# Tiles moved to the weights' address modulo 2048, and a bias table copied from DRAM instead of from SBUF: a two-layer decoder trunk

## The chip, the cores and the metric

One core of one Trainium2 chip runs the whole program. The time is device time in microseconds (us) of one execution; lower is better. The inputs and the outputs are in the chip's DRAM. The other names below are those of the profile: PE is TensorE's matmul, PEld its weight load, DVE is VectorE, ACT is ScalarE, POOL is GpSimd, SP is SyncE, whose queue issues most of the DMAs.

## The reference

The input is 512 tokens of width 1024. All is float32.

```python
def reference(x, ...):
    # layer 0
    x = x + hgrn2_mixer(rmsnorm(x, g0), w_in, w_out, ...)     # 8 heads, gated linear recurrence
    x = x + conv_ffn(rmsnorm(x, g1), w_up, conv, w_down)      # 1024 -> 2 x 2816 -> 1024
    # keys and values of layer 1 come from the stream here
    k, v = split(rmsnorm(x, g2) @ kv_w)
    # layer 1
    x = x + diff_attention(rmsnorm(x, g3), k, v, w_q, w_o, rel_table, ...)
    x = x + conv_ffn(rmsnorm(x, g4), w_up, conv, w_down)
    return rmsnorm(x, g5)

def conv_ffn(h, w_up, conv_w, conv_b, w_down):
    u = causal_depthwise_conv3(h @ w_up) + conv_b
    gate, val = split(u)
    return (silu(gate) * val) @ w_down

# diff_attention: per head two score maps, each softmax(q_c @ k_c.T + bias), out = (p_0 - lam * p_1) @ v;
# bias[h, i, j] = rel_table[t5_bucket(i - j), h], minus infinity where j > i
```

## The kernel before

**Layout.** The stream x is kept transposed: 8 tiles `x0` to `x7` of 128 channels by 512 tokens. A float32 product is made of three products of the rounded type F32R: each operand is split into a high and a low part, and `mm3` (lines 102 to 104) issues high by high, high by low, low by high. An operand that is split is named `..h` and `..l`: `xh`, `xl` for the normed stream, `yh`, `yl` for a mixer's output before its out-projection, `hh`, `hl` for the inner layer of the FFN (`hid` in the code, 22 pairs), `whi`, `wlo` for weights, `kh`, `kl` and `qs` for keys and queries.

**One matmul.** A projection's matmul has 128 columns of a weight tile as the stationary operand (512 bytes of each partition) and a whole 512-token tile as the moving operand (2048 bytes of each partition). One output tile takes 8 k-tiles by 3 matmuls from the stream, and 22 by 3 in the down-projection (`residual`). Values are the other way round: the weights move, 256 columns at a time, and the stream is stationary.

**Where tiles lie.** Pools are laid one behind the other in SBUF in the order in which they are opened: `const`, `weights`, `xsplit`, `small`, and then one pool per stage (`hgrn`, `ffn0`, `attn`, `ffn1`), each from where `small` ends. A pool's tags stand in the order of their first use, and every buffer is rounded up to 32 bytes. `weights` holds nine buffers of 4096 bytes and `xsplit` sixteen of 2048, so weights and the split stream have the same address modulo 2048. `small` ends with 22 buffers of 32 bytes, so the stages begin 704 bytes past that place. In `ffn` three tiles `u` of 2056 bytes (2080 when rounded up) come first, so `hid` begins 704 + 3 x 32 = 800 bytes past it. In `hgrn` the outputs `ys` come behind `dl`, `lb`, `om`, `scd`, `sd`, `oacc`, so 704 + 96 + 1024 = 1824 bytes past it. In `attn` the outputs `ys` begin 704 bytes past it, and keys and queries 160 bytes further.

**Weights.** `stage` (line 79) issues the DMA of a 512 KB weight tile into one of three `wst` buffers, all on SP's queue; `split` makes `whi` with ACT (line 57) and `wlo` with DVE (line 58), into three buffers each. In the attention, `Load` does the same with lines 756 and 759, and POOL multiplies the gain in (line 84).

**Order.** A scheduler orders `hgrn` and `ffn` from the program's order. The first matmuls, the attention and the last tile are in hand-written order. In `hgrn`, head h's projections and `prep` run ahead of the score products of head h - 1 (`intra`), and the gate's projection of head h - 2 fills in.

**The bias.** At head 2, `bias_vector` (line 702) makes a vector of 383 numbers for each of the 8 heads, in partitions 0 to 7 of one SBUF tile (`bvec`), and one DMA on SP's queue (line 711) writes each vector 128 times into a DRAM table, `bdram`, of 8 x 128 x 383 numbers: 1024 rows of 1532 bytes, 1.57 MB. The attention reads it at an offset that grows by one for each row (line 743), some 550 us later.

Of the kernel before, what the change touches and what calls it, by code (L numbers as in the profile page):

```python
# [11 lines left out]
F32 = mybir.dt.float32  # L12
F32R = mybir.dt.float32r
# [6 lines left out]
P = 128  # L20
T = 512
D = 1024
KD = D // P
NH = 8
DFF = 2816
KF = DFF // P
# [3 lines left out]
U0, U1, U2, U3 = 8, 2, 3, 1  # L30
PIECES = {0: 1, 1: 3, 3: 6, 6: 8}
WARM = 8


class Trunk:
# [237 lines left out]
    def hgrn(self, xs, acc, on_tile):  # L273
        tc, nc, a, sp = self.tc, self.nc, self.a, self.sp
        v, s = nc.vector, nc.scalar
        with ExitStack() as ctx:
            hp = ctx.enter_context(tc.tile_pool(name="hgrn", bufs=1))
            self.banks(ctx, "hgrn", mm=(4, 1), at=(4, 1))
            f_ps, q_ps = self.bank(), self.bank()
            self.begin(xs, acc, f_ps, q_ps)  # L280
            rb, rc = self.rstd(self.sums(acc, "at"), "n0", "at")
# [10 lines left out]
            for t in scd + sd:  # L292
                nc.gpsimd.memset(t, 0.0)
            oacc = hp.tile([P, T], F32, tag="oacc", name="oacc")
            ys = [(hp.tile([P, T], F32R, tag=f"yh{h}", name=f"yh{h}"),
                   hp.tile([P, T], F32R, tag=f"yl{h}", name=f"yl{h}")) for h in range(NH)]

            def big(tag, name, bufs):
                return hp.tile([P, T], F32, tag=tag, name=name, bufs=bufs)
# [203 lines left out]
            vt, pr, o = {}, {}, {}  # L503
# [145 lines left out]
    def ffn(self, layer, xs, acc, on_tile, final=None):  # L649
        tc, nc, a = self.tc, self.nc, self.a  # L650
        v, s = nc.vector, nc.scalar
        with ExitStack() as ctx:
            fp = ctx.enter_context(tc.tile_pool(name=f"ffn{layer}", bufs=1, reuse_waits="tile"))
            self.banks(ctx, f"ffn{layer}", mm=(8, 1))
            us = [fp.tile([P, T + 2], F32, tag=f"u{i}", name=f"u{i}") for i in range(3)]
            for u in us:
                nc.gpsimd.memset(u[:, 0:2], 0.0)
            hid = [(fp.tile([P, T], F32R, tag=f"hh{j}", name=f"hh{j}"),
                    fp.tile([P, T], F32R, tag=f"hl{j}", name=f"hl{j}")) for j in range(KF)]
            count = 0  # L660

            def conv(ps, n):
                nonlocal count
                u = us[count % 3]
                count += 1
                w = lambda i: self.cw[:, layer, i, n:n + 1]
                v.tensor_tensor(u[:, 2:], ps, rb, ALU.mult)  # L667
                c = fp.tile([P, T], F32, tag="c", name="c", bufs=3)
                s.activation(c, u[:, 2:], AF.Identity, bias=self.cb[:, layer, n:n + 1], scale=w(2))  # L669
                v.scalar_tensor_tensor(c, u[:, 1:T + 1], w(1), c, ALU.mult, ALU.add)  # L670
                v.scalar_tensor_tensor(c, u[:, 0:T], w(0), c, ALU.mult, ALU.add)  # L671
                return c

            def pair(j, pg, pv):
                cg = conv(pg, j)
                s.activation(cg, cg, AF.Silu)
                cv = conv(pv, KF + j)
                v.tensor_tensor(cv, cv, cg, ALU.mult)  # L678
                self.split(cv, *hid[j])

            up = a["w_up"][layer]
            first = [(self.bank("mm"), self.weights(up[n])) for n in range(3)]
            steps, got = self.norm_steps(acc, f"f{layer}", "mm")
            self.proj_first(first, xs, KD - 1, (lambda: None,) + steps)
            rb = got[1][0]
            ps3 = self.bank("mm")
            self.proj(ps3, self.weights(up[3]), xs, range(KD))
            pair(0, first[0][0], first[1][0])
            pair(1, first[2][0], ps3)
            for j in range(2, KF):  # L690
                pp = []
                for n in (2 * j, 2 * j + 1):
                    ps = self.bank("mm")
                    self.proj(ps, self.weights(up[n]), xs, range(KD))
                    pp.append(ps)
                pair(j, *pp)
            self.residual(a["w_down"][layer], hid, KF, on_tile, final=final)


    def bias_vector(self):  # L700

        nc, a = self.nc, self.a
        tab = self.sp.tile([P, T], F32, tag="sq", name="btab", bufs=2)
        nc.scalar.dma_start(tab[0:32, 0:NH + 384], a["rel"])
        u = self.sp.tile([P, T], F32, tag="sq", name="bvec", bufs=2)
        nc.scalar.dma_start(u[0:NH, 0:384], a["c_far"])
        ps = self.bank("at")
        nc.tensor.matmul(ps[:NH, :384], tab[0:32, 0:NH], tab[0:32, NH:NH + 384], start=True, stop=True)
        nc.vector.tensor_tensor(u[0:NH, 0:384], u[0:NH, 0:384], ps[:NH, :384], ALU.subtract)
        self.bdram = self.dp.tile([NH, P, 383], F32, tag="bdram", name="bdram")  # L710
        nc.sync.dma_start(self.bdram, u[0:NH, 0:383].unsqueeze(1).broadcast_to([NH, P, 383]))


    def attention(self, xkv, acc, on_tile):
        tc, nc, a = self.tc, self.nc, self.a
        v, s = nc.vector, nc.scalar
        mm = nc.tensor.matmul
        with ExitStack() as ctx:
            ap = ctx.enter_context(tc.tile_pool(name="attn", bufs=2, reuse_waits="tile"))
            self.banks(ctx, "attn", mm=(2, 1), sc=(4, 1), tp=(1, 1), po=(1, 1))  # L720
            def minus_lambda():
                lm = ap.tile([64, 4], F32, tag="lm", name="lm", bufs=1)
                nc.sync.dma_start(lm, a["lam"])
                pr = ap.tile([64, 2], F32, tag="lmp", name="lmp", bufs=1)
                v.tensor_tensor(pr, lm[:, 0:4:2], lm[:, 1:4:2], ALU.mult)
                pl = self.bank("mm")
                mm(pl[:, 0:2], self.ones[0:64, :], pr, start=True, stop=True)
                e = ap.tile([P, 2], F32, tag="lme", name="lme", bufs=1)
                s.activation(e, pl[:, 0:2], AF.Exp)
                d = ap.tile([P, 1], F32, tag="lmd", name="lmd", bufs=1)  # L730
                v.tensor_tensor(d, e[:, 1:2], e[:, 0:1], ALU.subtract)
                lam = ap.tile([P, 1], F32, tag="lam", name="lam", bufs=1)
                v.tensor_scalar(lam, d, -LAMBDA_INIT, None, ALU.add)
                return lam

# [72 lines left out]
            lam = minus_lambda()  # L808
# [140 lines left out]
            def scores(b):  # L949
                h, i = divmod(b, 4)  # L950
                if i == 0:
                    heads[h] = [ap.tile([P, 2, 4], F32, tag="sums", name="sums"),
                                ap.tile([P, 4], F32, tag="r0", name="r0"),
                                ap.tile([P, 4], F32, tag="oms", name="oms")]
                n = (i + 1) * P
                oi = slice(i * P, n)
                sc = [self.bank("sc")[:, :n] for c in range(2)]
                st = ap.tile([P, 2], F32, tag="stat", name="stat", bufs=4)
                pt = ap.tile([P, 2, T], F32, tag="p", name="p")
                for c in range(2):  # L960
                    mm(sc[c], qs[h][:, c, oi], ks[h][0][:, c, 0:n], start=True, stop=False)
                    mm(sc[c], qs[h][:, c, oi], ks[h][1][:, c, 0:n], start=False, stop=True)
                for c in range(2):
                    v.tensor_tensor_reduce(sc[c], sc[c], nbs[h // 2][:, h % 2, T - n:], 1.0, 3e38, ALU.add, ALU.min,  # L964
                                           st[:, c:c + 1])
                blocks[b] = pt

                def powers():
                    for c in range(2):
                        s.activation(pt[:, c, :n], sc[c], AF.Exp, bias=st[:, c:c + 1], scale=-1.0,  # L970
                                     accum_out=heads[h][0][:, c, i:i + 1])
                return powers

            def weigh(b):

                h, i = divmod(b, 4)
                n = (i + 1) * P
                sums, r0 = heads[h][:2]
                pt = blocks.pop(b)
                r1 = ap.tile([P, 2], F32, tag="r1", name="r1", bufs=4)  # L980
                v.reciprocal(r1[:, 0:1], sums[:, 1, i:i + 1])
                v.reciprocal(r0[:, i:i + 1], sums[:, 0, i:i + 1])
                v.scalar_tensor_tensor(r1[:, 1:2], sums[:, 0, i:i + 1], r1[:, 0:1], lam, ALU.mult, ALU.mult)
                at = blocks[b] = ap.tile([P, T], F32, tag="at", name="at")
                v.scalar_tensor_tensor(at[:, :n], pt[:, 1, :n], r1[:, 1:2], pt[:, 0, :n], ALU.mult, ALU.add)
# [24 lines left out]
            def close(h):  # L1010

                sums, r0, ms, po = heads.pop(h)
                o = ap.tile([P, T], F32, tag="o", name="o")
                me = ap.tile([P, 4], F32, tag="ome", name="ome")
                r = ap.tile([P, 4], F32, tag="or", name="or")
                by_token = o.rearrange("p (i x) -> p i x", i=4)

                def turn_back():
# [230 lines left out]
```

## Time and profile before

| what | value |
|---|---|
| median of 3 runs | 1283.47 us (1282.53 to 1287.66) |
| the profiled execution | 1283.88 us, span 1282.0 us |
| PE busy | 1246.9 us, 97% of the span |
| PEld busy | 1045.2 us, 82% |
| DVE busy | 869.2 us, 68% |
| ACT busy | 567.9 us, 44% |
| POOL busy | 111.1 us, 9% |
| DMA | 115.35 MB, mean 90 GB/s |

The span is that of the instructions; the execution's own time lies 1.9 us above it. Busy time of PE overstates its work, since matmuls are pipelined: each lasts some 0.39 us and the next begins some 0.23 us after it. So the pace of PE is read from start to start, or from the number of matmuls in a stretch, and not from its busy share.

### The profile page before, as it was taken

Reading aid. Unit: us, or ns where it says so; the run is one execution under the profiler, and the core shown is the slowest. Engines: PE = TensorE matmul, PEld = TensorE weight load, DVE = VectorE, ACT = ScalarE, POOL = GpSimd, SP = SyncE. Lnnn points to the kernel's source line nnn. Section 1 sums busy time; section 2 is a strip of 40 time slices with the busy share of each in tenths; the row PEclk is TensorE's granted clock in tenths of the full one; section 3 lists DMA queues with packets and bytes.
Section 4 is the critical chain, followed back from the end, with each engine's and each line's share of the span. In section 5 each row is a group of like instructions: output and inputs, shape, how many; then the busy total and the mean of one; then the engine's idle time right before and its main releaser. Section 6 shows DMA issues by size and latency. Waiting matters only on the chain.

```text
span 1282.0 us, 18032 instructions
## 1 busy us (share of the span) xinstructions
PE 1246.9 (97%) x6994; PEld 1045.2 (82%) x6994; DVE 869.2 (68%) x1627; ACT 567.9 (44%) x986; POOL 111.1 (9%) x93
## 2 busy tenths in 40 slices
PE   8999899999999999999999899999999999999997
PEld 7888698778888888888878788798788888888886
DVE  7978689676877777533357888876687777762223
ACT  5554455454444444322235546554454444442221
POOL 3000000020000000001143432200200000000001
PEclk9999899999999999999999899999999999999998
DMA  6225322132333333233322221222232333333321
GB/s 208 83 85 81 102 67 84 50 115 83 99 99 99 99 99 99 82 100 91 97 76 83 74 67 58 66 83 67 89 107 96 92 96 97 99 91 90 95 86 66
DMA packets 37949, 115.35 MB, mean 90 GB/s; under 512 B 4032, under 2 KB 9448, under 8 KB 37864
## 3 DMA queue, kind: packets, MB, share of 16 engines
q1 hardware_dynamic: 36968, 113.29, 29.6%
q8 instruction: 55, 0.90, 0.3%
q10 hardware_dynamic: 896, 0.92, 0.2%
q14 instruction: 30, 0.25, 0.1%
HBM read 110.52 MB, written 3.67 MB: 89 GB/s over the span
## 4 chain that ended last, share of the span: by engine, by line
PE 53%; issue 30%; DVE 11%; ACT 3%; DMA 2%; POOL 0%; SPq 0%; POOLq 0%; ACTq 0%; DVEq 0%
PE mm L103 15%; PE mm L102 15%; PE mm L104 15%; DMA wst<-in_w_fqg_dram 2%; DVE wlo L759 1%; DVE kl L857 1%; PE po L1005 1%; DVE wlo L58 1%; ACT whi L756 1%; DVE sd L457 1%; DVE sc L964 1%; PE tp L992 1%; DVE qs L840 1%; ACT p L970 0%; ACT whi L57 0%
## 5 line engine op out<-in xcount | busy, mean ns | idle before, releaser
L102 PE MATMUL mm<-xh,whi 128*128 128x512 f32 x1008 | 399.6, 396 | 0.4 <-ACT whi L57 0.4
L103 PE MATMUL mm<-xl,whi 128*128 128x512 f32 x1008 | 396.4, 393 | 3.0 <-DVE xl L61 2.9
L104 PE MATMUL mm<-xh,wlo 128*128 128x512 f32 x1008 | 396.0, 393 | 1.1 <-DVE wlo L58 1.1
L58 DVE TENSOR_TENSOR wlo<-wst,whi 128x1024 fp32r<-128x1024 f32 (+2 forms) x182 | 215.7, 1189 | 165.8 <-ACT whi L57 163.4
L57 ACT CAST whi<-wst 128x1024 fp32r<-128x1024 f32 (+2 forms) x182 | 181.8, 1003 | 257.9 <-PE mm L103 192.4
L103 PEld LDWEIGHTS mm<-xl,whi 128*128 128x128 f32 x1008 | 191.0, 190 | 42.4 <-DVE xl L61 4.5
L104 PEld LDWEIGHTS mm<-xh,wlo 128*128 128x128 f32 x1008 | 190.7, 189 | 42.2 <-DVE wlo L58 2.3
L102 PEld LDWEIGHTS mm<-xh,whi 128*128 128x128 f32 x1008 | 191.0, 190 | 38.8 <-ACT whi L57 1.2
L102 PE MATMUL mm<-hh,whi 128*128 128x512 f32 (+1 forms) x374 | 142.8, 382 | 0.0
L103 PE MATMUL mm<-hl,whi 128*128 128x512 f32 (+1 forms) x374 | 142.6, 381 | 0.0
L104 PE MATMUL mm<-hh,wlo 128*128 128x512 f32 (+1 forms) x374 | 142.6, 381 | 0.0
L667 DVE TENSOR_TENSOR u<-mm,rbc_f 128x512 f32<-128x512 f32 x88 | 60.2, 688 | 73.4 <-PE mm L104 73.4
L147 POOL TENSOR_TENSOR acc<-acc,sq 128x512 f32<-128x512 f32 x18 | 26.7, 1482 | 664.2 <-ACT sq L146 664.1
L102 PEld LDWEIGHTS mm<-hh,whi 128*128 128x128 f32 x374 | 70.1, 188 | 15.2
L104 PEld LDWEIGHTS mm<-hh,wlo 128*128 128x128 f32 x374 | 70.1, 188 | 15.2
L103 PEld LDWEIGHTS mm<-hl,whi 128*128 128x128 f32 x374 | 70.1, 188 | 15.1
L669 ACT ACTIVATE c<-u,pack 128x512 f32<-128x512 f32 x88 | 71.5, 816 | 7.7 <-DVE u L667 4.0
L102 PE MATMUL mm<-whi,xh 128*128 128x256 f32 x256 | 73.8, 290 | 0.0
L103 PE MATMUL mm<-wlo,xh 128*128 128x256 f32 x256 | 72.5, 283 | 0.6 <-DVE wlo L759 0.6
L57 ACT CAST hh<-c 128x512 fp32r<-128x512 f32 x44 | 27.2, 619 | 102.9 <-DVE c L678 102.9
L104 PE MATMUL mm<-whi,xl 128*128 128x256 f32 x256 | 72.4, 283 | 0.0
L671 DVE SCALAR_TENSOR_TENSOR c<-u,pack,c 128x512 f32<-128x512 f32 x88 | 66.1, 752 | 2.7
(259 smaller groups left out, 1717.0 us busy)
## 6 DMA issues: line engine op xcount, KB each, us to landing
wst<-in_w_up_dram SPq DMA_DIRECT2D x88, 512.0 KB, 3.6
wst<-in_w_down_dram SPq DMA_DIRECT2D x32, 512.0 KB, 3.5
wst<-in_w_fqg_dram SPq DMA_DIRECT2D x22, 512.0 KB, 4.1
wst<-in_w_kq_dram SPq DMA_DIRECT2D x16, 512.0 KB, 3.6
wst<-in_w_down_dram SPq DMA_DIRECT2D x16, 384.0 KB, 3.2
wst<-in_w_i_dram SPq DMA_DIRECT2D x8, 512.0 KB, 4.2
wst<-in_w_ao_dram SPq DMA_DIRECT2D x8, 512.0 KB, 4.0
wst<-in_w_v_dram SPq DMA_DIRECT2D x8, 512.0 KB, 3.6
```

What stands on the lines that cost most here:

```text
L57: i = nc.scalar.copy(hi, x)
L58: j = nc.vector.tensor_tensor(lo, x, hi.bitcast(F32), ALU.subtract)
L102: mm(out, s[0], m[0], start=start, stop=False)
L103: mm(out, s[0], m[1], start=False, stop=False)
L104: mm(out, s[1], m[0], start=False, stop=stop)
L147: add = lambda engine=nc.vector: engine.tensor_tensor(acc, acc, sq, ALU.add)
L457: v.copy_predicated(dst, m, src)
L667: v.tensor_tensor(u[:, 2:], ps, rb, ALU.mult)
L669: s.activation(c, u[:, 2:], AF.Identity, bias=self.cb[:, layer, n:n + 1], scale=w(2))
L671: v.scalar_tensor_tensor(c, u[:, 0:T], w(0), c, ALU.mult, ALU.add)
L756: s.copy(me.w[0], me.st)
L759: v.tensor_tensor(me.w[1], me.st, me.w[0].bitcast(F32), ALU.subtract)
```

## The change

Two things. First, tiles change their place. `ys` of `hgrn` and `hid` of `ffn` are made first in their pools. The attention's small tiles go from its own pool to `small`, and one of them gets 152 idle columns (`FILL`), so that `small` ends 2048 bytes past a multiple of 2048 from the weights (704 bytes, 640 for the padded `lm`, 704 for the others). The stages then begin at the weights' place modulo 2048, and `ys`, `hid`, `kh`, `kl` and `qs` lie there. Second, the bias vector goes to DRAM once (`once`, 12 KB), and the table is written from this copy, DRAM to DRAM, with a wait for the first DMA between the two. The arithmetic and the order of the calls stay.

```diff
+FILL = 152
@@ hgrn
             self.banks(ctx, "hgrn", mm=(4, 1), at=(4, 1))
+            ys = [(hp.tile([P, T], F32R, tag=f"yh{h}", name=f"yh{h}"),
+                   hp.tile([P, T], F32R, tag=f"yl{h}", name=f"yl{h}")) for h in range(NH)]
             f_ps, q_ps = self.bank(), self.bank()
...
             oacc = hp.tile([P, T], F32, tag="oacc", name="oacc")
-            ys = [(hp.tile([P, T], F32R, tag=f"yh{h}", name=f"yh{h}"),
-                   hp.tile([P, T], F32R, tag=f"yl{h}", name=f"yl{h}")) for h in range(NH)]
@@ ffn
+            hid = [(fp.tile([P, T], F32R, tag=f"hh{j}", name=f"hh{j}"),
+                    fp.tile([P, T], F32R, tag=f"hl{j}", name=f"hl{j}")) for j in range(KF)]
             us = [fp.tile([P, T + 2], F32, tag=f"u{i}", name=f"u{i}") for i in range(3)]
             for u in us:
                 nc.gpsimd.memset(u[:, 0:2], 0.0)
-            hid = [(fp.tile([P, T], F32R, tag=f"hh{j}", name=f"hh{j}"),
-                    fp.tile([P, T], F32R, tag=f"hl{j}", name=f"hl{j}")) for j in range(KF)]
@@ bias_vector
+        once = self.dp.tile([NH, 383], F32, tag="bonce", name="bonce")
+        nc.sync.dma_start(once, u[0:NH, 0:383])
         self.bdram = self.dp.tile([NH, P, 383], F32, tag="bdram", name="bdram")
-        nc.sync.dma_start(self.bdram, u[0:NH, 0:383].unsqueeze(1).broadcast_to([NH, P, 383]))
+        nc.sync.dma_start(self.bdram, once.unsqueeze(1).broadcast_to([NH, P, 383]))
@@ attention
-                lm = ap.tile([64, 4], F32, tag="lm", name="lm", bufs=1)
+                lm = self.sp.tile([64, 4 + FILL], F32, tag="lm", name="lm", bufs=1)[:, :4]
...
-                    heads[h] = [ap.tile([P, 2, 4], F32, tag="sums", name="sums"),
-                                ap.tile([P, 4], F32, tag="r0", name="r0"),
-                                ap.tile([P, 4], F32, tag="oms", name="oms")]
+                    heads[h] = [self.sp.tile([P, 2, 4], F32, tag="sums", name="sums"),
+                                self.sp.tile([P, 4], F32, tag="r0", name="r0"),
+                                self.sp.tile([P, 4], F32, tag="oms", name="oms")]
...
```

The lines left out do the same with `lmp`, `lme`, `lmd`, `lam`, `stat`, `r1`, `ome` and `or`.

## Rows read from the trace of the kernel before

**Rows 1.** Busy time in two stretches: HGRN, and most of the attention
```profile
core 0: us, PE busy (x) PEld busy (x) DVE busy (x) ACT busy (x) POOL busy (x), PEclk, DMA share, GB/s
0.00:250.00 250.00, 238.08 (x2171) 205.85 (x2171) 200.37 (x511) 127.67 (x270) 10.89 (x16) 0.98 0.36 97
...
650.00:850.00 200.00, 187.25 (x1123) 163.81 (x1121) 161.71 (x393) 108.67 (x278) 63.66 (x45) 0.97 0.22 69
```

**Rows 2.** The chain that ended last, in order of time: start us, us, what
```profile
81.78 0.67 PE at L439 x6
...
109.35 27.74 DMA wst<-in_w_fqg_dram
```

**Rows 3.** Waits, 94 to 140 us: total us, times, longest
```profile
ACT whi L57 <- DMA wst<-in_w_fqg_dram: 10.5, 1, 10.5
```

**Rows 4.** PE in order of time, 136 to 149 us: start us, us, what
```profile
136.37 0.39 PE L102 MATMUL mm<-xh,whi 128*128 128x512 f32 x1
142.05 1.65 PE L439 MATMUL at<-vt,kt 128*128 128x128 f32 x6 [5.29 <-ACT kt L436]
143.35 0.77 PE L103 MATMUL mm<-xl,whi 128*128 128x512 f32 x1
...
147.76 0.63 PE L104 MATMUL mm<-xh,wlo 128*128 128x512 f32 x1
148.19 0.44 PE L102 MATMUL mm<-xh,whi 128*128 128x512 f32 x1
```

**Rows 5.** DMA issues: KB each, median us from issue to landing
```profile
wst<-in_w_fqg_dram SPq DMA_DIRECT2D x22, 512.0 KB, 4.1
...
out_dram<-fin SPq DMA_DIRECT2D x6, 256.0 KB, 2.3
```

**Rows 6.** SP's queue in order of time, 94 to 135 us
```profile
101.52 0.83 SPq L711 DMA_DIRECT2D bdram<-bvec  x1
109.35 14.26 SPq L79 DMA_DIRECT2D wst<-in_w_fqg_dram  x3
```

**Rows 7.** Stretches (columns as in rows 1): table being written, stall, output being written
```profile
104.00:114.00 10.00, 10.00 (x49) 8.34 (x48) 10.00 (x29) 6.37 (x14) 0.00 (x0) 1.00 0.45 50
...
136.00:142.00 6.00, 0.76 (x4) 0.30 (x2) 3.68 (x7) 3.45 (x6) 0.00 (x0) 0.95 0.49 165
142.00:148.00 6.00, 5.95 (x17) 4.99 (x18) 6.00 (x23) 2.38 (x8) 0.00 (x0) 0.50 0.33 116
1272.00:1280.00 8.00, 1.72 (x8) 1.24 (x8) 4.07 (x22) 1.19 (x3) 1.57 (x3) 0.67 0.58 194
```

**Rows 8.** Stretches without a pause, weight loads alone: us, busy (count), PEclk, DMA
```profile
310.00:510.00 200.00, 165.62 (x883) 1.00 0.33 100
545.00:645.00 100.00, 80.31 (x429) 1.00 0.32 95
272.00:292.00 20.00, 16.12 (x86) 1.00 0.27 79
```

**Rows 9.** Same for the second FFN, all engines (columns as in rows 1)
```profile
955.00:1125.00 170.00, 170.00 (x752) 140.76 (x751) 123.38 (x157) 77.06 (x95) 0.00 (x0) 1.00 0.32 98
1155.00:1255.00 100.00, 100.00 (x433) 80.45 (x432) 29.03 (x31) 26.85 (x32) 0.00 (x0) 1.00 0.30 87
```

**Rows 10.** Groups of matmuls by line and shape: count, busy us, mean ns
```profile
L102 PE MATMUL mm<-hh,whi 128*128 128x512 f32 x330 | 130.4, 395 | 0.0
...
L102 PE MATMUL mm<-yh,whi 128*128 128x512 f32 x88 | 36.1, 410 | 0.0
...
L102 PE MATMUL mm<-hh,whi 128*128 128x256 f32 x44 | 12.5, 283 | 0.0
...
L102 PE MATMUL sc<-yh,whi 128*128 128x512 f32 x24 | 9.6, 402 | 0.0
...
L102 PE MATMUL at<-yh,whi 128*128 128x512 f32 x16 | 6.4, 411 | 0.0
```

**Rows 11.** Waits of PE, 640 to 910 us (columns as in rows 3)
```profile
PE tp L992 <- DVE at L985: 9.2, 5, 2.7
```

More of the change, by code (lines that the diff above doesn't have):

```diff
@@ L721, in minus_lambda @@
             def minus_lambda():
-                lm = ap.tile([64, 4], F32, tag="lm", name="lm", bufs=1)
+                lm = self.sp.tile([64, 4 + FILL], F32, tag="lm", name="lm", bufs=1)[:, :4]
                 nc.sync.dma_start(lm, a["lam"])
-                pr = ap.tile([64, 2], F32, tag="lmp", name="lmp", bufs=1)
+                pr = self.sp.tile([64, 2], F32, tag="lmp", name="lmp", bufs=1)
                 v.tensor_tensor(pr, lm[:, 0:4:2], lm[:, 1:4:2], ALU.mult)
@@ L727, in minus_lambda @@
                 mm(pl[:, 0:2], self.ones[0:64, :], pr, start=True, stop=True)
-                e = ap.tile([P, 2], F32, tag="lme", name="lme", bufs=1)
+                e = self.sp.tile([P, 2], F32, tag="lme", name="lme", bufs=1)
                 s.activation(e, pl[:, 0:2], AF.Exp)
-                d = ap.tile([P, 1], F32, tag="lmd", name="lmd", bufs=1)
+                d = self.sp.tile([P, 1], F32, tag="lmd", name="lmd", bufs=1)
                 v.tensor_tensor(d, e[:, 1:2], e[:, 0:1], ALU.subtract)
-                lam = ap.tile([P, 1], F32, tag="lam", name="lam", bufs=1)
+                lam = self.sp.tile([P, 1], F32, tag="lam", name="lam", bufs=1)
                 v.tensor_scalar(lam, d, -LAMBDA_INIT, None, ALU.add)
@@ L957, in scores @@
                 sc = [self.bank("sc")[:, :n] for c in range(2)]
-                st = ap.tile([P, 2], F32, tag="stat", name="stat", bufs=4)
+                st = self.sp.tile([P, 2], F32, tag="stat", name="stat", bufs=4)
                 pt = ap.tile([P, 2, T], F32, tag="p", name="p")
@@ L979, in weigh @@
                 pt = blocks.pop(b)
-                r1 = ap.tile([P, 2], F32, tag="r1", name="r1", bufs=4)
+                r1 = self.sp.tile([P, 2], F32, tag="r1", name="r1", bufs=4)
                 v.reciprocal(r1[:, 0:1], sums[:, 1, i:i + 1])
@@ L1013, in close @@
                 o = ap.tile([P, T], F32, tag="o", name="o")
-                me = ap.tile([P, 4], F32, tag="ome", name="ome")
-                r = ap.tile([P, 4], F32, tag="or", name="or")
+                me = self.sp.tile([P, 4], F32, tag="ome", name="ome")
+                r = self.sp.tile([P, 4], F32, tag="or", name="or")
                 by_token = o.rearrange("p (i x) -> p i x", i=4)
```

## The prediction

> **What bounds the kernel now.** I read the busy shares first, then the stretches by stage, the chain that ended last, and the waits. PE is busy 97% of the span and DVE 68%, so a microsecond counts only where PE loses it. The stretches show where that is: in HGRN PE is busy 238.08 of 250 us, in the attention 187.25 of 200, with a granted clock of 0.98 and 0.97 [rows 1]; both FFNs run without a gap [rows 9]. The chain shows one piece out of scale: a weight tile that took 27.74 us from issue to landing [rows 2], where its kind takes 4.1 [rows 5]. Behind it stands one wait of ACT, 10.5 us [rows 3], then a hole of PE of 5.29 us [rows 4] and a stretch at half clock [rows 7]. The second thing to see is PE's pace where nothing waits: 883 weight loads in 200 us are 226.5 ns for each matmul of the up-projection; 429 in 100 us are 233.1 in the down-projection; 86 in 20 us are 232.6 in the out-projection of HGRN [rows 8]. The second FFN repeats it: 751 loads in 170 us, 226.4, and 432 in 100, 231.5 (a few loads of half width shorten the mean, and one load too many stands in each stretch) [rows 9]. All these are matmuls of 512 columns at full clock.
>
> **The table's copy.** It is issued at 101.52 [rows 6] and reads 8 partitions of SBUF. While it runs alone, the DMA engines move 50 GB/s with 0.45 of 16 busy [rows 7]: 7.2 engines at 6.9 GB/s each. 1.57 MB at 50 GB/s are 31.4 us, from about 102.5 to 134. The weight tile issued at 109.35 stands behind it, and SP's three issues from there took 14.26 us together [rows 6], so the queue was backed up. The tile lands at 109.35 + 27.74 = 137.1, and ACT, which has waited for it since 126.6 (137.1 less 10.5 [rows 3]), splits it then.
>
> What this costs PE, from its rows in order of time [rows 4]: the last matmul before the hole starts at 136.37 and would be followed at 136.60. The clock is back at full speed with the matmul of 148.19. In these 11.59 us PE did six matmuls of line 439, which take 0.67 us in the head before [rows 2], and 11 of 512 columns (143.35 to 147.76, every 0.43 us), which take 2.50 us at 227 ns. [...] DVE is at 80% over the stage [rows 1], so it has room to do its part of this work earlier.
>
> How fast is the copy from DRAM? No row shows DRAM to DRAM. Reading weights from DRAM runs at 165 GB/s with 0.49 of 16 engines busy, 21 GB/s an engine; writing the output to DRAM at 194 with 0.58, again 21 [rows 7]. If reading and writing overlap, 7.2 engines move 151 GB/s: 10.4 us. If each row is read and then written, half that: 20.8 us. The lower end of the gain is that writing these rows, and not reading them, is what is slow: 31.4 us again. I take 10.4, since the plain rows on both sides are three times as fast as this copy, and what is different in it is the 8 source partitions. The wait for `once` is a DMA of 12 KB into DRAM; output DMAs land in 2.3 us [rows 5]. So the table's copy is issued near 104, starts near 105, and ends near 115.5, or 126 if serial. SP stands still for those 2.3 us; the next weight issue behind it comes at 109.35 [rows 6], when its buffer is free, so nothing is held. That tile then lands 2 us behind the copy, near 117.5, nine before ACT turns to it at 126.6. No stall is left up to a copy of some 20 us; serial copying leaves about 1 us. Gain: **8.4 us**, with ends 0 (less the 2.5 us that the copy starts later) and 8.4.
>
> [...]
>
> **The place of the tiles.** In the up-projection the moving tiles (`xh`, `xl`) lie at the weights' place modulo 2048; `hid` lies 800 bytes off, `ys` of HGRN 1824, `ys` of the attention 704. Shape, clock and order of the three products are the same. The difference in pace is 233.1 - 226.5 = 6.6 ns. DVE is busier in the faster stretch, 123.38 of 170 us against 29.03 of 100 [rows 9], and so is the DMA by a little, so neighbours' work doesn't explain it. I take it that place does, and that moved tiles run at the pace of `xh`. Then:
> - down-projections: 330 x 3 = 990 matmuls [rows 10] x 6.6 ns = 6.5 us;
> - out-projection of HGRN: 64 of the 88 + 24 + 16 = 128 matmuls of line 102 [rows 10], x 3 = 192, x 6.1 ns (232.6 - 226.5) = 1.2 us;
> - out-projection of the attention: also 192. Half run after the heads, where I count 96 x 6.6 = 0.6 us; half between the heads, where PE also waits for DVE (9.2 us on line 985 alone [rows 11]), so 0 to 0.6; I take 0.
> - the last tile's 44 x 3 = 132 matmuls of 256 columns [rows 10], of another shape: not priced by these rows; at 6.6 ns either way 0.9 us, taken as 0.
> - scores: keys and queries already have one common place before; only their neighbours' changes. 0, with 0.5 either way.
> Sum: **8.3 us**, with ends 0 (place isn't the cause) and some 10.
>
> [...]
>
> **The rest.** The small tiles moved into `small` no longer share space with the first FFN, so they wait for nothing new; their count of buffers stays. `hid` now lies over the outputs `ys` of the stage before, whose last readers are the out-projections, over before the first `hid` is written some 15 us into the FFN. These are counted at nothing. In the attention the start of work shifts, and its holes and half-clock stretches can come or go: at 0.97 of the clock over 200 us [rows 1] some 6 us of clock are missing there, and 12.75 us of PE are idle. I take 0, with 5 either way.
>
> **The sum.** The profiled execution, 1283.88 us, less 8.4 and 8.3, is 1267.2. It lay 0.4 us above the median of the runs, so the forecast is **1267 us**. A measurement of this kernel can tell about 0.5%, 6.4 us, from no change.
>
> **The rivals.**
> - [...] Chance 0.11.
> - *The copy stays slow* because writing 1024 rows to DRAM from 8 engines, or reading one row 128 times, is the limit: the stall stays and begins 2.5 us later, 1283.5 - 8.3 + 2.5 = 1278. Against: 21 GB/s an engine on either side [rows 7]. Chance 0.07.
> - *Given back in the attention*: it waits for DVE there, and PE arriving elsewhere meets a longer hole and a further half-clock stretch: 1267 + 5 = 1272. Chance 0.10. The opposite, its holes shrinking, gives 1262; chance 0.10.
> - [...] Nothing in the rows shows reads of one place; chance 0.03.
> - The forecast: 0.59.
>
> The bound for faster is 1277.1, for slower 1289.9. Faster: 0.59 + 0.11 + 0.20, and 0.01 of the slow copy: 0.91. Slower 0.03, same 0.06. The likeliest case alone spans 1264 to 1270; the range takes in the attention's 5 us on the fast side with the unpriced ends, and the two rivals of 1275 and 1278 on the other: 1260 to 1278.
>
> **What would show it.** Right: the weight tile issued near 109 lands within 12 us and the hole of PE near 136 and its half clock are gone; 100 us of either down-projection hold about 441 weight loads in place of 429; the up-projections are unchanged. Wrong: 429 again (place is nothing), a DMA of over 20 us left in the chain near 105 to 130 (the copy is slow), or new holes of PE in the attention that eat more than 5 us.

## The result, and the profile after

The changed kernel takes **1267.87 us** (median of 4 runs, 1266.55 to 1269.33) against 1283.0 before: a ratio of 0.9872, with an interval of 0.9857 to 0.9887. The forecast was 1267. The profiled execution is 1269.33 us, span 1267.5, 14.5 us below the span before.

The copy first. SP's queue in order of time, changed kernel:

```profile
101.10 0.35 SPq L713 DMA_DIRECT2D bonce<-bvec  x1
102.50 0.76 SPq L715 DMA_DIRECT2D bdram<-bonce  x1
108.91 22.73 SPq L81 DMA_DIRECT2D wst<-in_w_fqg_dram  x5
```

The wait between the two copies holds the queue for 1.4 us, and nothing is issued in the next 6 us. The last line merges five issues from the start of the first to the end of the last; it isn't the time that they took. The issues of weights from line 81 in the same stretch, as a group:

```profile
L81 SPq DMA_DIRECT2D wst<-in_w_fqg_dram x6: 327/328/351, 97.6 to 131.3; - x6
...
DMA to landing us min/median/max: 3.7/3.8/7.2
```

Before, the slowest of them landed after 27.74 us [rows 2] and three issues, one right behind the other, took 14.26 us together [rows 6]; now none takes over 0.351 us to issue, and the slowest lands after 7.2. Two stretches of the same kernel, the columns as in rows 1: the table being written, and the place where PE had its hole.

```profile
104.00:114.00 10.00, 10.00 (x49) 8.37 (x48) 10.00 (x28) 6.34 (x13) 0.00 (x0) 1.00 0.59 184
136.00:142.00 6.00, 6.00 (x31) 5.07 (x30) 5.97 (x23) 3.22 (x7) 0.00 (x0) 1.00 0.00 0
```

184 GB/s stand where 50 stood (155 of them are rows of the table, a weight tile moves beside them), and 6.00 us of PE with a granted clock of 1.00 where 0.76 us stood [rows 7]. In the trace's DMA packets a row of 1532 bytes takes a median of 65 ns where it took 228. The table's rows run from 104.0 to 114.3 us, 10.3 us at 152 GB/s; the forecast was 10.4 us at 151, ending near 115.5.

The pace next: weight loads alone, in the up-projection, both down-projections and the out-projection of HGRN.

```profile
310.00:510.00 200.00, 165.59 (x883) 1.00 0.32 97
530.00:630.00 100.00, 82.81 (x442) 1.00 0.32 98
1140.00:1230.00 90.00, 74.53 (x398) 1.00 0.33 97
255.00:275.00 20.00, 16.57 (x89) 1.00 0.38 124
```

The up-projection has the 883 loads that it had [rows 8]; the down-projection has 442 in 100 us where it had 429, and the out-projection 89 in 20 where it had 86. Taken from start to start, which no window's edge falsifies, the pace of `hid` goes from 233.3 to 226.7 ns, the pace of the up-projection.

Where the 14.5 us came from, by the starts of matmuls in one profiled execution of each kernel (an out- or down-projection is from its first matmul to its last, the up-projection from there to the first of `hid`; "heads" is from the first to the last score matmul with `kh`):

| stage | before | after | table alone | place alone |
|---|---|---|---|---|
| HGRN up to its out-projection | 237.0 | 228.0 | 230.0 | 238.5 |
| of it, from the score products of the fourth head on | 108.1 | 99.5 | 99.6 | 108.1 |
| out-projection of HGRN | 51.1 | 50.2 | 52.6 | 51.8 |
| up-projection, first FFN | 241.1 | 241.0 | 241.1 | 241.0 |
| down-projection, first FFN | 123.0 | 119.5 | 123.0 | 119.5 |
| attention, heads | 195.6 | 197.9 | 193.5 | 193.6 |
| rest of the attention's out-projection | 36.5 | 36.0 | 36.5 | 36.0 |
| down-projection, second FFN | 124.9 | 122.2 | 124.9 | 122.2 |

The last two columns belong to the first two experiments. The second row begins at one and the same matmul, 128.94 us before, ahead of the old hole. That matmul comes 0.4 us earlier in the changed kernel and 1.5 later in each of the two others; this shift is there in the first head already, near 46 us, before the copy is issued, so it isn't the stall's. The out-projection of HGRN is 1.5 and 1.6 us longer in the last two columns than in the first two: a stretch of 3.4 us at half clock lies in it (from 237.8 and from 247.9 us). The rows left out (the start of the attention, the second up-projection, the end) differ by 1.9 us at most.

### The profile page after: what moved, and what is told of

Read it like the earlier page. It is cut to its first block, busy times and chain, and to the rows that moved or that the text cites. A ratio compares the mean times of both kernels' runs of the same rounds, so it can differ in the third digit from the quotient of the medians.

```text
span 1267.5 us, 18031 instructions
## 1 busy us (share of the span) xinstructions
PE 1235.7 (97%) x6994; PEld 1043.4 (82%) x6994; DVE 872.0 (69%) x1627; ACT 569.1 (45%) x986; POOL 110.0 (9%) x93
## 4 chain that ended last, share of the span: by engine, by line
PE 57%; issue 30%; DVE 9%; ACT 2%; DMA 0%; SPq 0%; POOL 0%; POOLq 0%; ACTq 0%; DVEq 0%
PE mm L106 16%; PE mm L104 16%; PE mm L105 16%; DVE wlo L763 1%; PE po L1009 1%; DVE wlo L60 1%; DVE kl L861 1%; DVE sc L968 1%; PE tp L996 1%; ACT whi L760 1%; PE sc L104 1%; PE sc L105 1%; PE sc L106 1%; DVE sd L459 1%; DVE qs L844 1%
```

## The experiments

**The two halves, each alone.** Theory: 8.4 us lie in the copy and 8.3 in the place, and the two don't touch. Rival: one of them carries the whole gain. `table_only` is the kernel before with

```diff
+        once = self.dp.tile([NH, 383], F32, tag="bonce", name="bonce")
+        nc.sync.dma_start(once, u[0:NH, 0:383])
         self.bdram = self.dp.tile([NH, P, 383], F32, tag="bdram", name="bdram")
-        nc.sync.dma_start(self.bdram, u[0:NH, 0:383].unsqueeze(1).broadcast_to([NH, P, 383]))
+        nc.sync.dma_start(self.bdram, once.unsqueeze(1).broadcast_to([NH, P, 383]))
```

> The kernel before with the table's copy from DRAM alone; all tiles stay where they were. If the two halves of the change are independent, as the prediction's sum has it: 8.4 us less than before, 1274.6 us; the hole of PE near 136 us and the half clock behind it are gone; 100 us of the first down-projection still hold 429 weight loads. Rival: the whole gain hangs on the stall (the later stages being faster for another reason, such as the small tiles' pool): then about 1268.

and `place_only` is the changed kernel with this edit undone.

> The changed kernel with the table's copy from the SBUF vector as before. If independent: 8.3 us less than before, 1274.7 us; the weight tile issued near 109 us takes 27 us again, PE has its hole and half clock again; 100 us of either down-projection hold 441 weight loads. Rival: the stall is larger or smaller because PE comes to it at another moment: 1270 to 1279.

Measured: 1273.7 us (ratio 0.9934, 0.9914 to 0.9954) and 1275.16 us (0.9943, 0.9924 to 0.9961). Stretches of `table_only`: the place of the old hole, then (weight loads alone) the down-projection.

```profile
134.00:140.00 6.00, 6.00 (x31) 5.08 (x30) 6.00 (x23) 2.36 (x8) 0.00 (x0) 1.00 0.32 104
...
545.00:645.00 100.00, 80.36 (x429) 1.00 0.31 94
```

The hole is gone and the pace is the old one. The same of `place_only`, with 10 us more ahead:

```profile
124.00:134.00 10.00, 7.66 (x133) 7.42 (x132) 1.52 (x5) 2.15 (x5) 0.00 (x0) 1.00 0.45 49
134.00:140.00 6.00, 1.51 (x41) 1.45 (x41) 0.00 (x0) 0.54 (x1) 0.00 (x0) 0.60 0.49 137
...
545.00:645.00 100.00, 82.81 (x442) 1.00 0.34 98
```

The hole is back, with the half clock behind it, and the pace is the new one. The slowest weight tile of the stretch lands after 28.6 us, as it did after 27.74. The waits, 94 to 140 us of `place_only`:

```profile
ACT whi L59 <- DMA wst<-in_w_fqg_dram: 11.4, 1, 11.4
PE at L421 <- issue: 6.8, 1, 6.8
```

ACT waits for the same DMA as before [rows 3]. PE's own hole is put down to "issue" this time: nothing that its semaphores show released it. The DMA packets show a likely reason. Queue q8 carries 55 packets of kind "instruction" (16384 bytes) in each of these traces. The eighth starts at 121.99 us before and at 123.42 in `table_only`, after 1971 of PE's matmuls and weight loads in both; in `place_only` it starts at 136.18, after 2241, while PE stands still, and PE goes on at 138.49. So here the table's copy seems to have held up PE's instructions beside the weight tile, if q8 carries them: the trace names no engine for it, and that it is PE's is an estimate from these counts. How the price divides between the two is open. The price isn't: from the fourth head on HGRN takes 8.6 us more than in the changed kernel.

The gains of the two halves are 9.7 and 8.3 us, by their medians against the 1283.43 of the kernel before beside them: a sum of 18.0, where both at once gave 15.1. By the intervals the halves gain 5.9 to 11.0 and 5.0 to 9.8, so the difference of 2.9 isn't clear of noise, and the traces can't place it: the profiled executions of the halves are the slowest of their four, and their spans gain 5.9 and 5.1. In its own stages each half gains alone what it gains in the change, to 0.2 us (the table's second, fifth and last two rows; the out-projection of HGRN has its half clock). The rival is out.

**Which place, against what?** Theory: the place of the moving tile against the stationary one sets the pace. Rivals: the stage sets it; the address itself does. `x_apart` puts 800 bytes between the weights and all that follows:

```diff
+        self.gp = ctx.enter_context(tc.tile_pool(name="gap", bufs=1))
+        self.gap = self.gp.tile([P, 200], F32, tag="gap", name="gap")
+        tc.nc.gpsimd.memset(self.gap, 0.0)
         self.xp = ctx.enter_context(tc.tile_pool(name="xsplit", bufs=2 * KD))
```

> The changed kernel with 800 idle bytes between the weights and all that follows: the split stream, the inner layer, the outputs lie 800 bytes off the weights' place, and at one place among themselves. If the place against the weights sets the pace: every matmul of 512 columns of the projections goes from 226.5 to 233.1 ns, some 4400 of them, 29 us more than the changed kernel, 1297 us; matmuls of 256 columns unknown. Rival, the pace is a matter of the stage (what else runs in it): the up-projections stay at 226.5 and the time at 1268. Rival, what counts is that the moving tiles lie at one place among themselves: 1268.

`all_shifted` has the same three lines ahead of the pool of the weights instead.

> The changed kernel with 800 idle bytes ahead of the weights, so that weights, stream, inner layer and outputs all move by 800 bytes and keep their place against each other. If the place against the weights sets the pace: 1268 us, 226.5 ns everywhere. Rival, the absolute address modulo a power of two sets it: 233 ns in all projections, 1297 us.

Measured: 1290.13 us for `x_apart`, slower than the kernel before (ratio 1.0053, 1.0038 to 1.0068), and 1267.54 us for `all_shifted` (0.9877, 0.9861 to 0.9894). Weight loads alone in `x_apart`, first up- and down-projection, second up-projection; then the first two in `all_shifted`:

```profile
310.00:510.00 200.00, 160.63 (x857) 1.00 0.31 95
545.00:645.00 100.00, 80.35 (x429) 1.00 0.32 96
960.00:1130.00 170.00, 136.57 (x729) 1.00 0.31 94
```

```profile
310.00:510.00 200.00, 165.68 (x883) 1.00 0.31 98
530.00:630.00 100.00, 82.84 (x442) 1.00 0.33 100
```

857 loads in 200 us are 233.4 ns: the up-projection, with its stage and neighbours untouched, is now as slow as the down-projection was. Moving everything changes nothing. Both rivals are out. The expected 1297 was 7 too high. Two pieces of it show in the trace: matmuls of 256 columns in the values became faster (a median of 117 to 118 ns for 120); and in the attention, where other matmuls stand between, the projections from the stream ran at 230.1 ns (the mean of steps between 200 and 260) and not 226.7 at the weights' place as well, so that going to 232.8 cost 2.7 there.

**How far must it agree?** Three scans make the first tile of `ys` and two of `hid` wider and use their last 512 columns:

```diff
-            hid = [(fp.tile([P, T], F32R, tag=f"hh{j}", name=f"hh{j}"),
+            pad = {0: (8, 32)[layer], KF // 2: (8, 32)[layer]}
+            hid = [(fp.tile([P, T + pad.get(j, 0)], F32R, tag=f"hh{j}", name=f"hh{j}")[:, -T:],
```

This is the first scan: 32 and 64 bytes in the first FFN, 128 and 256 in the second, with 512 for `ys` of HGRN by the same means.

> The changed kernel with idle bytes inside the stages' pools, so that the inner layer of the first FFN lies 32 bytes past the weights' place in its first 11 pairs and 64 in the others, that of the second FFN 128 and 256, and the outputs of HGRN 512 past it. The pace is read from the trace, in runs of 33 matmuls of 512 columns. If only the same place modulo 2048 is fast: 233.3 ns at all five. If what counts is the place modulo 512, the length of a stationary slice: 226.7 at 512 and 233.3 at the others. If it is the place modulo a line of some tens of bytes: 226.7 at the larger ones too. If the place is a scale and not a switch: other numbers than these two. Time: 1268 to 1276 us.

> As in the first scan, with 480 and 448 bytes in the first FFN, 384 and 192 in the second, 1024 for the outputs of HGRN. Modulo 2048: 233.3 ns at all five. Modulo 512: 226.7 at 1024 and 233.3 at the others. A scale: other numbers, the same for 32 and 480 if it counts the distance to the nearest multiple of 512. Time: 1268 to 1276 us.

> As in the first two scans, with 96 and 160 bytes in the first FFN, 224 and 96 in the second, 160 for the outputs of HGRN. The scans so far gave 226.7 ns at 0, 256, 512 and 1024 bytes, 228.8 at 64, and 233.3 at 32, 128, 192, 384, 448, 480. If the pace has a period of 256 bytes and 0 is its best place: none of these below 226.7. Rival: one of them is faster than the weights' own place.

Times of one run each: 1271.63, 1271.56 and 1273.06 us. The pace is the mean from start to start over matmuls 7 to 31 of each run of 33 (for HGRN, and for the kernel before in the attention, over all steps between 200 and 260 ns, and there the median stands). One step more or less at the ends of a run moves a mean by up to 0.2:

| bytes past the weights' place | ns |
|---|---|
| 0 (changed kernel) | 226.7 |
| 32 / 64 / 96 | 233.2 / 228.8 / 233.2 to 233.5 |
| 128 / 160 / 192 / 224 | 233.3 / 234.2 / 233.2 / 233.3 |
| 256 | 226.5 |
| 384 / 448 / 480 | 232.8 / 233.4 / 233.3 |
| 512 / 1024 (HGRN) | 227 / 227 |
| 704 / 800 (kernel before) | 233 / 233.3 |

Weight loads in order of time, first scan, first FFN, 20 steps at 64 bytes and 20 at 32:

```profile
544.87 0.19 PEld L105 LDWEIGHTS mm<-hl,whi 128*128 128x128 f32 x1
...
549.45 0.19 PEld L104 LDWEIGHTS mm<-hh,whi 128*128 128x128 f32 x1
...
552.21 0.19 PEld L104 LDWEIGHTS mm<-hh,whi 128*128 128x128 f32 x1
...
556.88 0.19 PEld L106 LDWEIGHTS mm<-hh,wlo 128*128 128x128 f32 x1
```

4.58 us are 229 ns a step, 4.67 are 233.5. All of the scans' multiples of 256 are fast, everything else is slow but 64, which lies between. So 2048 is more than is needed, and the pace isn't a plain switch. No place beats the weights' own. `modulo_256` uses this:

```diff
-FILL = 152
+FILL = 24
```

> The changed kernel with 24 idle columns in place of 152, so that all stages begin 1536 bytes past the weights' place, a multiple of 256 and not of 2048. Period of 256 bytes: 226.7 ns in the projections and the changed kernel's time, 1268 us. Modulo 2048 as the change has it: 233.3 ns in the down- and out-projections, 1276 us.

Measured: 1266.47 us (0.987, 0.9853 to 0.9886). Weight loads alone, down-projection:

```profile
530.00:630.00 100.00, 82.81 (x442) 1.00 0.33 98
```

All stages begin 1536 bytes past the weights' place, and the pace and the time are those of the changed kernel. A period of 256 bytes is thus shown for the places tried.

**Why was the copy slow?** Theory: eight neighbouring source partitions; from eight others the copy is then as fast as from DRAM, and the time is that of the changed kernel. Rival: an SBUF source that is read 128 times. `ports` makes the vectors in partitions 0, 4, ... 28 and writes the table from there, with no copy to DRAM:

```diff
...
+        wide = self.sp.tile([P, T], F32, tag="res", name="wide", bufs=1)
+        nc.gpsimd.memset(wide[0:32, 0:32], 0.0)
+        nc.vector.tensor_copy(wide[0:32, 0:32:4], tab[0:32, 0:NH])
-        nc.tensor.matmul(ps[:NH, :384], tab[0:32, 0:NH], tab[0:32, NH:NH + 384], start=True, stop=True)
+        nc.tensor.matmul(ps[:32, :384], wide[0:32, 0:32], tab[0:32, NH:NH + 384], start=True, stop=True)
...
-        nc.sync.dma_start(self.bdram, once.unsqueeze(1).broadcast_to([NH, P, 383]))
+        nc.sync.dma_start(self.bdram, u[0:32:4, 0:383].unsqueeze(1).broadcast_to([NH, P, 383]))
```

> The changed kernel without the copy to DRAM: the eight bias vectors are made in partitions 0, 4, 8, ... 28 instead of 0 to 7 (a matmul with 32 columns, 24 of them zero), and the table is written from these by one DMA, SBUF to DRAM, still 1024 rows of 1532 bytes. [...] Rival, any SBUF source of few partitions (or this one that repeats) is slow: 31 us, the stall is back, 1275 us.

Measured: 1268.11 us (0.9881, 0.9864 to 0.9898). The stretch in which the table is written:

```profile
104.00:114.00 10.00, 10.00 (x49) 8.36 (x49) 10.00 (x33) 4.98 (x12) 0.00 (x0) 1.00 0.60 204
```

204 GB/s, a weight tile among them (154 are rows of the table), and 71 ns a row in the packets against 228 from partitions 0 to 7, with the same source memory, the same 1024 rows and the same writes. The rival is out: which partitions were read made the copy slow.

**Matmuls of 256 columns.** In the second scan's last tile, a moving operand at 192 bytes took 113 ns, against 120 at 0 and 116.7 at 800 before. `values_192` gives the weight buffers 256 bytes more and puts the values' weights, the moving operand there, 192 bytes further:

```diff
-    def weight_tiles(self):
-        return (self.wp.tile([P, 1024], F32R, tag="whi", name="whi"),
+    def weight_tiles(self, off=0):
+        return (self.wp.tile([P, 1088], F32R, tag="whi", name="whi")[:, off:off + 1024],
...
-                me.w = self.weight_tiles()
+                me.w = self.weight_tiles(48 if me.cols == 256 else 0)
```

> The changed kernel with weight buffers 256 bytes longer, in which the weights of the value projections (the moving operand there, 256 columns) lie 192 bytes further, so 192 bytes past the stationary stream modulo 256; everything else keeps its place modulo 256. In the last tile of the second scan, matmuls of 256 columns took 113.3 ns with a moving operand at 192, against 120 at 0. If it is the same with the roles of stream and weights turned round: 768 matmuls by 6.7 ns, 5 us at most, some of it hidden in the attention: 1263 to 1265 us. Rival, the rule holds for neither this order nor this place: 120 ns and 1268 us, or slower.

Measured: 1265.76 us (0.9858, 0.9844 to 0.9873). A value matmul takes a median of 117 ns in HGRN, 118 in the attention, not 113: some 3 ns by 768, 2.3 us. It is 2.1 us below the changed kernel, and 0.7 below `modulo_256`, with intervals that overlap: a better time isn't shown.

## Why the prediction was right, step by step

**The stall.** It named the copy as the reason of the late weight tile, and 8.4 us as its price: 11.59 us less the 0.67 and 2.50 of work done in them, some 5.5 in the hole from 136.60 to 142.05 [rows 4] and the rest at a granted clock of 0.50 [rows 7]. HGRN became shorter by 9.0 us in the changed kernel and by 7.0 with the table alone; from the fourth head on, past the shift at the start, it is 8.6 and 8.4. In `table_only` and `ports` the wait of ACT on the DMA and the hole are gone. The estimate of 10.4 us of copying, from the rates of reading and writing DRAM, met 10.3. For reading and writing that overlap speak the 65 ns a row: by an estimate from 1532 bytes and the forecast's 21 GB/s an engine a row takes 73 ns, and 146 if it is read and then written. Before, 7 or 8 rows were in flight in 27.1 of the 32.5 us, beside the 7.2 busy engines of the forecast. The wait for `once` cost 1.4 us of the queue, not 2.3. The source partitions made the difference: partitions 0 to 7 gave 50 GB/s [rows 7], eight partitions four apart 204, of which 48 and 154 are rows of the table.

**The place.** Term by term: the first down-projection gave 3.5 us (528 matmuls of the 990, 3.5 forecast), the second 2.7 of 3.0. The missing 0.4 is the last tile, which the prediction left unpriced: its 132 matmuls of 256 columns went from 116.7 to 120 ns. The out-projection of HGRN gave 0.9 of 1.2, the end of the attention's 0.5 of 0.6. That the place is the cause, which the prediction took from three slow stretches and two fast ones, is shown by `x_apart` and `all_shifted`. 6.7 ns a matmul depend on where the two operands lie to each other: in the up-projection 200 us held 857 loads in `x_apart` and 883 in `all_shifted`. Why they do, no run shows.

**The attention.** It was taken as 0, with 5 either way; in the profiled execution it gave back 2.3 us in the heads. This can't be put down to the change: with tiles at the same places modulo 256, the heads took 197.9 us in the changed kernel, 196.8 in `ports`, 193.6 in `modulo_256` and 192.9 in `all_shifted`, one execution each. In the first two the records of the granted clock hold 10.2 us at half clock there, in the other two 6.8; the kernel before had 10.2 as well. But `place_scan_2` has none there and took 193.5, so half clock alone doesn't explain the lengths. Why the heads are longer in one kernel than in the next wasn't tried.

**The number.** The stall gave 8.6 for 8.4 and the place 7.6 for 8.3: the mechanisms and nearly the sizes were right. That the time came within 1 us of the forecast is partly luck, since the start (up to 1.9 us between kernels) and the heads (up to 5.0) vary by more. The range also counts 1275, the time with the stall's gain alone: `table_only`, which has that alone, took 1273.7. For a kernel slower than before, counted with 0.03, no run shows a cause: the copy from DRAM moved its rows at 152 GB/s.

## What to carry to other kernels

Compare PE's pace from start to start between stages with the same shapes before asking what it waits for: a difference of 6.7 ns with no wait, over some 1300 matmuls, was here nearly as much (7.6 us) as the largest stall (8.6). Where float32 matmuls of full width alternate with weight loads, try the moving tiles at the stationary tiles' place modulo 256 bytes (here 226.7 ns where most other places gave 233), and look at narrower matmuls separately. A small broadcast from a few neighbouring partitions can hold up what is moved after it, here a weight tile that landed after 27.74 us, and it seems a block of instructions: write it once to DRAM, or spread its source over partitions, and look at the landing time of the transfer behind it.

## What the runs showed that was not expected

The cost of the place comes in steps of the same size at most places. In the half-clock stretch of the kernel before (143.92 to 147.76 us, granted clock 0.50 [rows 7]) matmuls of 512 columns start every 426.7 ns. Half of this, 213.3 ns, is an estimate for a granted clock of 1.00, and half again, 106.7, one for 256 columns. The measured paces lie above these estimates by 13.3 (226.7) and 20.0 (233.3) for 512 columns and by 13.3 (120.0), 10 (116.7) and 6.7 (113.3) for 256, all multiples of 3.3 ns. The place that is best for 512 columns is not so for 256: nothing tried was slower than its 120.0, and 192 bytes gave 113.3. For 256 columns the place alone doesn't set the pace: at 128 bytes it was 120.0 ns in one tile and 118.8 in the next.

After another kind of matmul a run took some steps to reach its even pace: in the attention of the changed kernel, at the weights' place, a run of 30 began with steps of 314, 233, 236, 224, 231, 236, 228, 233 and 230 ns, and then went on at 226 and 227. At 64 bytes, alone among the places off a multiple of 256, the pace was 228.8.
